# A nested set of seven quarter products in one of the seven block products of the down projection

## The chip, the cores and the metric

The kernel runs on one core of one Trainium2 chip. The metric is the device time of one execution in microseconds (us), the median of the runs shown. The engines are named as in the profile: PE multiplies matrices (PEld is its loading of weights), DVE and ACT work on vectors, POOL is a third engine that hardly matters here, and SP issues most DMA transfers.

## The reference

A decoder block over 1024 positions and 1024 channels in float32: a mixer (pooling and windowed attention), then an MLP. Only the MLP is touched by the change:

```python
h2 = _rmsnorm(x, g_mlp_pre[l])
ff = jnp.einsum('bsf,fd->bsd',
                jnp.square(jax.nn.relu(jnp.einsum('bsd,df->bsf', h2, w_up[l]))), w_down[l])
x = x + _rmsnorm(ff, g_mlp_post[l])
```

`w_up` is 1024 x 4096 and `w_down` 4096 x 1024. Below, f is the squared ReLU (1024 positions x 4096), the input of the down projection.

## The kernel before

**Three passes.** Every float32 matrix is split into a high part (a cast on ACT, L101) and a low part (a subtraction on DVE, L104), both in a rounded float32 format. A product is made in three passes of PE (`PASSES`, L32): high x high, high x low, low x high. A split's operand is ready when DVE has made its low part.

**Seven products for eight.** The matrix products of the MLP are made by blocks: the positions are halved, the columns are halved, the inner dimension is halved, and seven products of sums of blocks replace eight products of blocks. The seven are added up in a fixed scheme, in which later products are accumulated onto earlier ones in the PSUM banks where possible.

**The up part** goes over pairs of blocks of 128 columns of f. The class `Pairs` loads a pair's weights (L524, on SP's queue), makes their sums (L533 to L543), splits them (into tiles named wh and wx), and runs its seven products on PE (L584). The results are squared on ACT (L1613). The function `store` inside `up_close0` (L1615 to L1628) makes three sums of a pair's blocks of f, which the down part needs as left operands (s1, s2 and s4), and stores all to `f_dram` in DRAM. Its stores go to the same SP queue as the next pair's weight loads.

**The down part** is one list of steps: seven products in the order `PRODUCTS` (1, 5, 2, 3, 6, 7, 4), each in `NS` = 8 steps of 256 rows of the inner dimension. A step multiplies a left operand of 128 x 2 x 512 (the f sums, read back from `f_dram`, tile raw) by a right operand of the same size (blocks of `w_down` or differences of them, tiles B). `operands(i, s_)` issues the load, makes the difference of blocks of w where there is one, and splits both: the left into two slots of the pool wh (6 slots), the right into two of the pool ar (6 slots). It is called two steps ahead (`AHEAD`). `down_mm` then issues 24 matmuls of 128 x 128 by 128 x 512, that is 2 parts of the inner dimension x 4 tiles of 128 positions x 3 passes. A product is 192 matmuls. PSUM has two groups of four banks, "mm" and "at"; products 2 and 3 accumulate onto 1 and 5, the others start a group afresh.

Product 6, the fifth in the list, multiplies s2 by B22 - B11. After it, for each of the four tiles of positions, DVE adds the result to u (L2106), adds u to c12 (L2107) and to v (L2108), and multiplies c12 by a gain (L1991). Product 7 has DVE write B22 - B12 over B12's tile, and product 4 uses B21 - B11; its B21 blocks are loaded at L1966 into slots of the pool w (24 slots) that earlier blocks have left, and subtracted at L1967.

**Order.** Outside stretches whose order is written by hand, a scheduler of the framework places the instructions on each engine when the kernel is built. On the chip each engine then works through its list in that order, and an instruction that must wait (for data, or for a slot to be read for the last time) holds up all behind it on the same engine. That also holds for SP and its DMA issues.

Of the kernel before, what the change touches and what calls it, by code (L numbers as in the profile page):

```python
# [8 lines left out]
F32 = mybir.dt.float32  # L9
# [41 lines left out]
def block_kernel(ctx: ExitStack, tc, xt, x, consts, vecs, sinks, b_qkv, g_post, g_mlp, g_mlp_post,  # L51
# [1558 lines left out]
    def up_close0(m, f):  # L1610

        act.activation(f[:, 512:], f[:, 512:], AF.Relu)
        act.activation(f, f, AF.Square)  # L1613

        def store():  # L1615

            g = f_odd.pop(m + 1)
            t = g32([2, 512])
            s4 = (g32([S]) if m < 2 * NF0 else bcp.tile([P, S], F32, tag="bc", name=nm("s4")))[:, :512]
# [3 lines left out]
            dve.tensor_tensor(s4, g[:, :512], t[:, 1, :], ALU.subtract)  # L1623
# [7 lines left out]
    stores = []  # L1631

    def flush():
        while stores:
# [279 lines left out]
    dl = ctx.enter_context(tc.tile_pool(name="dl", bufs=16, reuse_waits="tile"))  # L1914

    def acc4(name):
        return [dl.tile([P, 512], F32, tag="acc", name=nm(name), bufs=16) for _ in range(4)]

    def raw_tile():
        return dl.tile([P, 2, 512], F32, tag="raw", name=nm("raw"), bufs=4)  # L1920
# [16 lines left out]
    def operands(i, s_):  # L1937

        if i == 1 and s_ in early_raw:
            ft, wt = early_raw[s_]  # L1940
        else:
            ft = stage([2, 512]) if (i, s_) == (1, 3) else raw_tile()
            nc.sync.dma_start(ft, f_block(A_OF[i], s_))
            if i == 1:
                resident("B11", s_)
                if s_ - 3 in early_raw:
                    resident("B11", s_ - 3)
                wt = res["B11", s_]
            elif i == 5:
                resident("B12", s_)  # L1950
                wt = res["B11", s_]
                dve.tensor_tensor(wt, res["B12", s_], wt, ALU.subtract)
            elif i == 2:
                wt = streamed("B21", s_)
            elif i == 3:
                resident("B22", s_)
                wt = res["B22", s_]
            elif i == 6:
                wt = res["B11", s_]
                dve.tensor_tensor(wt, res["B22", s_], wt, ALU.subtract)  # L1960
            elif i == 7:
                wt = res["B12", s_]
                dve.tensor_tensor(wt, res["B22", s_], wt, ALU.subtract)
            else:
                wt = rp.tile([P, 2, 512], F32, tag="w", name=nm("B21"))
                nc.sync.dma_start(wt, w_block("B21", s_))  # L1966
                dve.tensor_tensor(wt, wt, res["B11", s_], ALU.subtract)  # L1967
# [8 lines left out]
        opers[i, s_] = fo, wo_  # L1976

    def down_mm(i, s_, bs, after, order, last=(NS - 1, 1)):
        for s2, k2, t in order:
# [51 lines left out]
    def last_tile(i, n, b, order):  # L2031

        t = n - 4
        sums = small(2, "sq")
        b2 = bank("mm", [256])
        for h, o in ((0, b[:, :256]), (1, b2)):
            c = slice(h * 256, (h + 1) * 256)
            for s2, k2, _ in order:  # L2040
                fo, wo_ = opers[i, s2]
                for j, (fh, wh) in enumerate(PASSES):
                    pe.matmul(o, fo[fh][:, k2, t * P:(t + 1) * P], wo_[wh][:, k2, c],
                              start=h == 1 and k2 == 0 and j == 0, stop=k2 == 1 and j == 2, skip_group_check=h == 0)
# [20 lines left out]
    PRODUCTS = (1, 5, 2, 3, 6, 7, 4)  # L2065
    LATE = 3
# [5 lines left out]
    u, v, c11, c12 = acc4("u"), acc4("v"), acc4("c11"), acc4("c12")  # L2072
    banks = {}
    AHEAD = 2
    for j in range(1, AHEAD):
        operands(*steps[j])
    for j, (i, s_) in enumerate(steps):
        if j + AHEAD < len(steps):
            operands(*steps[j + AHEAD])
        if s_ == 0 and i not in (2, 3):  # L2080
            tag = "mm" if i in (5, 7) else "at"
            banks[i] = [bank(tag) for _ in range(4)]
        bs = banks[{2: 1, 3: 5}.get(i, i)]
# [4 lines left out]
        if i != 4 or s_ < NS - LATE:  # L2088
            down_mm(i, s_, bs, i in (2, 3), [(s_, k2, t) for k2 in range(2) for t in range(4)
                                             if (i, s_, t) != (4, NS - LATE - 1, 3)])  # L2090
            if s_ < NS - 1:
                continue
        elif s_ < NS - 1:
            continue
        for t in range(4):
# [7 lines left out]
            elif i == 3:  # L2103
                act.copy(c12[t], bs[t])
            elif i == 6:
                dve.tensor_tensor(u[t], u[t], bs[t], ALU.add)  # L2106
                dve.tensor_tensor(c12[t], c12[t], u[t], ALU.add)  # L2107
                dve.tensor_tensor(v[t], v[t], u[t], ALU.add)  # L2108
                fin_half(t, 1, c12[t])
# [104 lines left out]
```

## Time and profile before

| what | us |
|---|---|
| three runs | 1093.69, 1094.36, 1095.04 |
| median | 1094.36 |
| the profiled execution | 1093.78 |
| its span on the core | 1092.0 |
| PE busy | 1082.5 |
| DVE busy | 810.4 |
| ACT busy | 610.8 |

The span runs from the core's first instruction to its last; 1.8 us of the execution lie around it. In the trace's rows, a name such as `wh<-raw` is the tile written and the tiles read, `x12` is a run of twelve like instructions, and a bracket at the end says how long the engine stood idle before the row and what it waited for. An instruction's duration overlaps the next one's start by up to a tenth of a us on DVE and ACT, so the distance from start to start is what counts where instructions stand in a queue.

### The profile page before, as it was taken

The page shows a single profiled execution, that of the slowest core. Times are in us where ns is not written, and L with a number is a line of the kernel's source. Part 1 is how long each engine was busy: PE and PEld are TensorE (multiplying, and loading weights), DVE is VectorE, ACT ScalarE, POOL GpSimd, SP SyncE. Part 2 cuts the span into 40 slices and gives each one's busy share as a digit, 9 for nine tenths or more (in the row PEclk, how much of TensorE's full clock was granted, in tenths as well). Part 3 has the DMA queues.
Part 4 walks back from the last instruction along what each step waited for, and adds up shares of the span by engine and source line. Part 5 has one row for each costly group of instructions (what it writes and reads, how often), then busy time and mean ns, then how long its engine had stood idle before and what let it go on. Part 6 is the DMA issues. An engine that isn't in the chain of part 4 may idle for free.

```text
span 1092.0 us, 13883 instructions
## 1 busy us (share of the span) xinstructions
PE 1082.5 (99%) x5066; PEld 899.1 (82%) x5066; DVE 810.4 (74%) x1111; ACT 610.8 (56%) x1001; POOL 84.2 (8%) x142
## 2 busy tenths in 40 slices
PE   9999999999999999999999999999999999999997
PEld 8888888888888888888888888888888888888886
DVE  6689888999797887889867665655457866557685
ACT  7557886466654257457665564555346535435461
POOL 0344311100100012100000000000000000000000
PEclk9999999999999999999999999999999999999999
DMA  9858899679865776732565535345697886632622
GB/s 337 189 142 212 212 247 349 189 242 319 255 214 173 225 182 154 270 117 81 180 212 212 193 125 191 127 161 186 223 389 278 298 261 194 195 117 78 212 77 77
DMA packets 98612, 221.02 MB, mean 202 GB/s; under 512 B 10224, under 2 KB 27760, under 8 KB 98544
## 3 DMA queue, kind: packets, MB, share of 16 engines
q1 hardware_dynamic: 82256, 183.56, 50.2%
q0 software_dynamic: 10528, 16.78, 8.6%
q10 hardware_dynamic: 5760, 19.79, 4.8%
q8 instruction: 39, 0.64, 0.2%
q14 instruction: 29, 0.24, 0.1%
HBM read 158.24 MB, written 60.82 MB: 201 GB/s over the span
## 4 chain that ended last, share of the span: by engine, by line
PE 95%; DVE 2%; ACT 2%; DMA 0%; issue 0%; DVEq 0%; ACTq 0%; SPq 0%
PE mm L584 26%; PE at L584 18%; PE at L1982 15%; PE mm L1982 12%; PE mm L1516 5%; PE mm L495 3%; PE sc L183 2%; PE at L1244 2%; PE at L1516 2%; PE mm L192 2%; PE mm L1244 1%; PE mm L183 1%; PE mm L497 1%; PE sc L457 1%; PE sc L389 1%; PE at L1562 1%
## 5 line engine op out<-in xcount | busy, mean ns | idle before, releaser
L1982 PE MATMUL at<-ar,wh 128*128 128x512 f32 x696 | 159.0, 389 | 0.0
L1982 PEld LDWEIGHTS at<-ar,wh 128*128 128x128 f32 x696 | 130.6, 188 | 27.5 <-DVE ar L104 0.4
L1982 PE MATMUL mm<-ar,wh 128*128 128x512 f32 x576 | 131.0, 389 | 0.0
L1982 PEld LDWEIGHTS mm<-ar,wh 128*128 128x128 f32 x576 | 108.1, 188 | 22.5
L104 DVE TENSOR_TENSOR wh<-raw,wh 128x1024 fp32r<-128x1024 f32 x50 | 61.1, 1223 | 68.4 <-ACT wh L101 68.2
L101 ACT CAST wh<-raw 128x1024 fp32r<-128x1024 f32 x50 | 52.6, 1052 | 104.0 <-PE at L1982 51.6
L104 DVE TENSOR_TENSOR wh<-st,wh 128x512 fp32r<-128x512 f32 (+1 forms) x103 | 74.8, 736 | 30.0 <-ACT wh L101 25.5
L584 PE MATMUL mm<-T,wx 128*128 128x512 f32 x375 | 90.4, 389 | 0.0
L584 PEld LDWEIGHTS mm<-T,wx 128*128 128x128 f32 x375 | 70.4, 188 | 14.6
L584 PE MATMUL mm<-gr,wh 128*128 128x512 f32 x321 | 77.2, 391 | 0.0
L101 ACT CAST wh<-st 128x512 fp32r<-128x512 f32 (+2 forms) x102 | 65.7, 653 | 19.3 <-PE at L584 5.6
L584 PEld LDWEIGHTS mm<-gr,wh 128*128 128x128 f32 x321 | 59.9, 188 | 12.2
L584 PE MATMUL mm<-T,wh 128*128 128x512 f32 x267 | 66.1, 389 | 0.0
L104 DVE TENSOR_TENSOR ar<-B,ar 128x1024 fp32r<-128x1024 f32 x43 | 52.5, 1220 | 9.8 <-ACT ar L101 9.4
L584 PE MATMUL at<-gr,wh 128*128 128x512 f32 x243 | 59.0, 389 | 0.0
L584 PE MATMUL mm<-x,wh 128*128 128x512 f32 x240 | 58.9, 394 | 0.0
L584 PEld LDWEIGHTS mm<-T,wh 128*128 128x128 f32 x267 | 50.1, 188 | 10.4
L584 PEld LDWEIGHTS at<-gr,wh 128*128 128x128 f32 x243 | 45.6, 188 | 9.5
L584 PEld LDWEIGHTS mm<-x,wh 128*128 128x128 f32 x240 | 44.2, 188 | 9.6 <-ACT f L693 0.2
L584 PE MATMUL at<-T,wx 128*128 128x512 f32 x213 | 52.0, 389 | 0.0
L101 ACT CAST ar<-B 128x1024 fp32r<-128x1024 f32 x43 | 45.1, 1050 | 12.2 <-DMA B<-in_w_dn_dram 9.4
L584 PEld LDWEIGHTS at<-T,wx 128*128 128x128 f32 x213 | 40.0, 188 | 8.3
(510 smaller groups left out, 2127.0 us busy)
## 6 DMA issues: line engine op xcount, KB each, us to landing
raw<-f_dram SPq DMA_DIRECT2D x52, 512.0 KB, 3.9
B<-in_w_dn_dram SPq DMA_DIRECT2D x32, 512.0 KB, 6.7
f_dram<-g SPq DMA_DIRECT2D x28, 512.0 KB, 3.3
st<-in_w_up_dram SPq DMA_DIRECT2D x24, 512.0 KB, 4.7
g<-spill_dram SPq DMA_DIRECT2D x17, 512.0 KB, 5.7
f_dram<-g ACTq DMA_DIRECT2D x17, 512.0 KB, 2.6
st<-in_w_g_dram SPq DMA_DIRECT2D x16, 512.0 KB, 4.9
g<-in_w_up_dram SPq DMA_DIRECT2D x15, 512.0 KB, 5.9
```

The source lines that it names most:

```text
L101: act.copy(hi, src)
L104: eng.tensor_tensor(lo, src, f32(hi), ALU.subtract)
L183: pe.matmul(bq, xs_[k][n // 4][:, xh, n % 4 * P:(n % 4 + 1) * P], wq[k][:, h, :], start=k == 0 and j == 0, stop=k == NK - 1 and j == 2)
L192: pe.matmul(bkv_of(n), xs_[k][n // 4][:, xh, n % 4 * P:(n % 4 + 1) * P], wkv[k // 2][:, h, k % 2, :], start=k == 0 and j == 0 and not (joi ...
L389: pe.matmul(sb[:, kv, i, :nk], qt[r, qx, m * P:(m + 1) * P], kx[r, k0:k0 + nk], start=j == 0, stop=j == 2)
L457: pe.matmul(yb[:, kv], v[:, c:c + P], p[ph][:, 4 * kv:4 * kv + 4].rearrange("p i q -> p (i q)"), start=j < 2, stop=j >= len(mms) - 2)
L495: pe.matmul(bs[th], whi[:, k, :], rhs(k, hl, th), start=k == 0 and hl == 0, stop=False)
L497: pe.matmul(bs[th], wlo[:, k, :], rhs(k, 0, th), start=False, stop=k == nk - 1)
L584: pe.matmul(b, w[wh][:, kt, :], x_, start=not after and kt == 0 and j == 0, stop=kt == 3 and j == 2, skip_group_check=after)
L1244: pe.matmul(b, w[wh][:, kt, :], xo[xh][:, kt, :], start=not after and kt == 0 and j == 0, stop=kt == 1 and j == 2, skip_group_check=after)
L1516: pe.matmul(bs[t], Am[a][k][ah][:, t * P:(t + 1) * P], Wm[w][k][wh], start=not after and k == 0 and j == 0, stop=k == 3 and j == 2, skip_g ...
L1982: pe.matmul(bs[t], fo[fh][:, k2, t * P:(t + 1) * P], wo_[wh][:, k2, :], start=not after and s2 == 0 and k2 == 0 and j == 0, stop=(s2, k2) ...
```

## The change

Product 6 is itself made as seven products of quarters. s2 and B22 - B11 are halved once more in each direction: positions in two halves of 256, the inner rows of a step in two of 128, columns in two of 256. Per step there are seven products, each with 2 tiles of positions x 3 passes = 6 matmuls of 128 x 128 by 128 x 256: 42 in place of 24 of 512 columns.

- Left operands: the four quarters of s2 (`f1`) and three sums of quarters (`f2`). The sums run over two pairs of blocks of the up part. `store` makes the first half in even pairs (L1628) and the rest in odd pairs (L1633 to L1635), and puts them into the scratch tensor `spill`, 384 KB for each of the eight steps.
- Right operands: four quarters of B22 - B11, of which three are used as they are (`w1`), and four sums T (L2006 to L2008, `w2`).
- Splits of a step: f2 (768 columns), w2 (1024), w1 (512 and 256), f1 (1024), in place of two of 1024.
- Four of the seven quarter products start from zero in "at" banks; products 2, 3 and 4 accumulate onto three quarters of u that ACT copies into "mm" banks first (`ONTO`). `quarters_close` adds them up in u: one copy on ACT and eight additions on DVE. The four additions of L2106 go.
- Products 7 and 4 change their groups of banks ("at" for 7, "mm" for 4), and the tail's `b2` goes to "at".
- The last step and the closing are in an order written by hand, and product 7's operands are called for after it.

```diff
@@ store (up part)
+            if m // 2 % 2 == 0:
+                dve.tensor_tensor(s2[:, 256:], s2[:, :256], s2[:, 256:], ALU.subtract)
+                s2_even.append(s2)
+            else:
+                a = s2_even.pop()
+                e = g32([3, 256])
+                dve.tensor_tensor(e[:, 1, :], s2[:, 256:], a[:, 256:], ALU.subtract)
+                dve.tensor_tensor(e[:, 0, :], e[:, 1, :], a[:, :256], ALU.add)
+                dve.tensor_tensor(e[:, 2, :], s2[:, :256], e[:, 1, :], ALU.subtract)
+                q.dma_start(e_dram(m // 4), e)
             q.dma_start(fd[:, 4:6, :], t)
...
@@ operands
+        if i == QUARTERED:
+            quarters(s_, ft, wt)
+            return
...
+    def quarters(s_, ft, wt):
+        fs, w = raw_tile_of([3, 256]), halved(wt)
+        nc.sync.dma_start(fs, e_dram(s_))
+        tt = rp.tile([P, 4, 256], F32, tag="w", name=nm("T"))
+        dve.tensor_tensor(tt[:, 0:2, :], w[:, 1::2, :], w[:, 0:2, :], ALU.subtract)
+        dve.tensor_tensor(tt[:, 2, :], w[:, 3, :], tt[:, 0, :], ALU.subtract)
+        dve.tensor_tensor(tt[:, 3, :], w[:, 2, :], tt[:, 2, :], ALU.subtract)
+        f2, w2 = [wslot([3, 256]) for _ in range(2)], [ar([4, 256]) for _ in range(2)]
+        split(*f2, fs)
+        split(*w2, tt)
+        w1, f1 = [ar([4, 256]) for _ in range(2)], [wslot([4, 256]) for _ in range(2)]
+        for k in (slice(2, 4), slice(0, 1)):
+            split(w1[0][:, k, :], w1[1][:, k, :], w[:, k, :])
+        split(*f1, halved(ft))
+        opers[QUARTERED, s_] = f1, f2, w1, w2
+
+    PARTS = {1: (0, 0, 2, 0), 2: (0, 2, 2, 2), 3: (1, 2, 2, 3), 4: (0, 3, 3, 3), 5: (1, 0, 3, 0), 6: (1, 1, 3, 2),
+             7: (0, 1, 3, 1)}
+    ONTO = {2: (0, 0), 3: (0, 1), 4: (2, 0)}
...
+    def quarters_mm(s_):
+        o = opers[QUARTERED, s_]
+        order = (5, 6, 1, 7, 3, 2, 4) if s_ == 0 else (1, 6, 7, 5, 2, 3, 4) if s_ == NS - 1 else (5, 6, 3, 1, 2, 7, 4)
...
+        for q in order:
+            fs, fk, ws, wk = PARTS[q]
+            for t in range(2):
+                for j, (fh, wh) in enumerate(PASSES):
+                    pe.matmul(part[q][:, t, :], o[fs][fh][:, fk, t * P:(t + 1) * P], o[ws][wh][:, wk, :],
+                              start=q not in ONTO and (s_, t, j) == (0, 0, 0), stop=(s_, t, j) == (NS - 1, 1, 2),
+                              skip_group_check=q in ONTO)
+
+    def quarters_close():
+        (a, c), (d, e) = ([h[:, k] for k in range(2)] for h in (stage([2, 2, 256]), stage([2, 2, 256])))
+        act.copy(a, part[1])
+        dve.tensor_tensor(c, a, part[6], ALU.add)
+        dve.tensor_tensor(d, c, part[7], ALU.add)
+        dve.tensor_tensor(e, c, part[5], ALU.add)
+        w = block_of(u4, 2, 1)
+        dve.tensor_tensor(w, w, d, ALU.add)
+        dve.tensor_tensor(w, w, part[5], ALU.add)
+        for q, s in ((2, a), (3, e), (4, d)):
+            dve.tensor_tensor(block_of(u4, *ONTO[q]), s, part[q], ALU.add)
...
@@ the loop over steps
     for j, (i, s_) in enumerate(steps):
-        if j + AHEAD < len(steps):
+        closing = (i, s_) == (QUARTERED, NS - 1)
+        if j + AHEAD < len(steps) and not closing:
             operands(*steps[j + AHEAD])
...
+        if closing:
+            with tc.manual_schedule(engines=CORE):
+                quarters_mm(s_)
+                quarters_close()
+            operands(*steps[j + AHEAD])
...
             elif i == 6:
-                dve.tensor_tensor(u[t], u[t], bs[t], ALU.add)
                 dve.tensor_tensor(c12[t], c12[t], u[t], ALU.add)
```

Where the instructions stand now on the engines is seen in three places. First, DVE around the start of product 6, after the change (numbers behind names tell tiles apart; L1984 is the subtraction B21 - B11, which was L1967, and raw with 768 columns is the stored sum of quarters):

```order
L104 TENSOR_TENSOR wh_8204<-raw_8197,wh_8203 128x768
L104 TENSOR_TENSOR ar_8206<-T_8199,ar_8205 128x1024
L104 TENSOR_TENSOR ar_8212<-B_1085_7088,ar_8211 128x512
L104 TENSOR_TENSOR ar_8212<-B_1085_7088,ar_8211 128x256
L1984 TENSOR_TENSOR B_1422_9116<-B_1422_9116,B_1085_7088 128x1024
L104 TENSOR_TENSOR wh_8214<-raw_8194,wh_8213 128x1024
L1984 TENSOR_TENSOR B_1428_9153<-B_1428_9153,B_1092_7126 128x1024
L104 TENSOR_TENSOR wh_8255<-raw_8248,wh_8254 128x768
L104 TENSOR_TENSOR ar_8257<-T_8250,ar_8256 128x1024
```

The first four and the sixth row are step 0's splits, the last two belong to step 1: the second subtraction of L1984, with a load of its own in front of it, stands between them.

Second, DVE around the end of product 6, before and after. Before (the first two rows are the splits of product 7's step 1; u, c and v are the sums named above):

```order
L104 TENSOR_TENSOR wh_8476<-raw_8472,wh_8475 128x1024
L104 TENSOR_TENSOR ar_8478<-B_1119_7264,ar_8477 128x1024
L2106 TENSOR_TENSOR u_6979<-u_6979,at_8234 128x512
L2106 TENSOR_TENSOR u_6980<-u_6980,at_8235 128x512
L2107 TENSOR_TENSOR c_1063_6991<-c_1063_6991,u_6979 128x512
L2108 TENSOR_TENSOR v_6983<-v_6983,u_6979 128x512
L2107 TENSOR_TENSOR c_1064_6992<-c_1064_6992,u_6980 128x512
L2108 TENSOR_TENSOR v_6984<-v_6984,u_6980 128x512
L1991 TENSOR_TENSOR c_1063_6991<-c_1063_6991,bc_6964 128x512
```

After, with the eight additions of the closing (L2045 to L2052) and a B21 subtraction among them, and the splits of product 7's step 1 (wh_8837, ar_8839):

```order
L1984 TENSOR_TENSOR B_1460_9334<-B_1460_9334,B_1098_7162 128x1024
L2046 TENSOR_TENSOR st_8822<-st_8821,at_8330 128x512
L2047 TENSOR_TENSOR st_8822<-st_8821,at_8327 128x512
L2049 TENSOR_TENSOR u_7027<-u_7027,st_8822 128x2x256
L104 TENSOR_TENSOR wh_8837<-raw_8833,wh_8836 128x1024
L2050 TENSOR_TENSOR u_7027<-u_7027,at_8327 128x2x256
L2052 TENSOR_TENSOR u_7027<-st_8821,mm_8333 128x2x256
L2052 TENSOR_TENSOR u_7027<-st_8822,mm_8331 128x2x256
L2052 TENSOR_TENSOR u_7027<-st_8822,mm_8335 128x2x256
L104 TENSOR_TENSOR ar_8839<-B_1123_7309,ar_8838 128x1024
L2193 TENSOR_TENSOR c_1067_7036<-c_1067_7036,u_7027 128x512
```

Before, step 1 of product 7 was split ahead of the additions, and step 2's first split stood behind sixteen additions and multiplications, four for each tile. After, step 1's splits stand among the closing's additions, and twelve more additions and multiplications stand between them and step 2's.

Third, SP's queue in an odd pair of the up part, after the change (L1636 stores the sums of quarters, L524 loads weights):

```order
L1637 DMA f_dram<-g_5183 128x1024
L1638 DMA f_dram<-g_4624 128x1024
L1636 DMA spill_dram<-g_5189 128x768
L1639 DMA f_dram<-g_5184 128x512
L524 DMA g_5247<-in_w_up_dram 128x1024
```

The new store stands in front of the weight load that before followed directly upon three stores.

More of the change, by code (lines that the diff above doesn't have):

```diff
@@ L1629, in up_close0, with e_dram @@
         stores.append(store)
-    stores = []
+    stores, s2_even = [], []
+    def e_dram(s_):
+        return spill[s_][:, :768].rearrange("p (a b) -> p a b", b=256)
     def flush():
@@ L1916, in acc4, with raw_tile_of @@
     def acc4(name):
-        return [dl.tile([P, 512], F32, tag="acc", name=nm(name), bufs=16) for _ in range(4)]
+        return [dl.tile([P, 512], F32, tag="acc", name=nm(name), bufs=12) for _ in range(4)]
+    def raw_tile_of(shape):
+        return dl.tile([P] + shape, F32, tag="raw", name=nm("raw"), bufs=4)
     def raw_tile():
-        return dl.tile([P, 2, 512], F32, tag="raw", name=nm("raw"), bufs=4)
+        return raw_tile_of([2, 512])
     sq = sp.tile([P, 2, NT], F32, tag="fsq", name="fsq", bufs=1)
@@ L1976, in operands, with halved @@
         opers[i, s_] = fo, wo_
+    def halved(t):
+        return t.rearrange("p k (a b) -> p (k a) b", b=256)
+    def quarters(s_, ft, wt):
[13 more added lines that the diff above has]
+        opers[QUARTERED, s_] = f1, f2, w1, w2
@@ new lines, in block_kernel, with block_of @@
+    PARTS = {1: (0, 0, 2, 0), 2: (0, 2, 2, 2), 3: (1, 2, 2, 3), 4: (0, 3, 3, 3), 5: (1, 0, 3, 0), 6: (1, 1, 3, 2),
+             7: (0, 1, 3, 1)}
+    ONTO = {2: (0, 0), 3: (0, 1), 4: (2, 0)}
+    part = {}
+    def block_of(t4, r, j):
+        return t4[:, r:r + 2, j * 256:j * 256 + 256]
+    def quarters_mm(s_):
+        o = opers[QUARTERED, s_]
+        order = (5, 6, 1, 7, 3, 2, 4) if s_ == 0 else (1, 6, 7, 5, 2, 3, 4) if s_ == NS - 1 else (5, 6, 3, 1, 2, 7, 4)
+        if s_ == 0:
+            for q in (5, 6, 1, 7, 3, 2, 4):
+                part[q] = bank("mm" if q in ONTO else "at", [2, 256])
+                if q in ONTO:
+                    act.copy(part[q], block_of(u4, *ONTO[q]))
+        for q in order:
[5 more added lines that the diff above has]
+                              skip_group_check=q in ONTO)
@@ L2065, in block_kernel @@
     PRODUCTS = (1, 5, 2, 3, 6, 7, 4)
+    QUARTERED = 6
     LATE = 3
@@ L2071, in block_kernel @@
     steps = [(i, s_) for i in PRODUCTS for s_ in range(NS)]
-    u, v, c11, c12 = acc4("u"), acc4("v"), acc4("c11"), acc4("c12")
+    u4 = dl.tile([P, 4, 512], F32, tag="u4", name="u4", bufs=1)
+    u, v, c11, c12 = [u4[:, t, :] for t in range(4)], acc4("v"), acc4("c11"), acc4("c12")
     banks = {}
@@ L2077, in block_kernel @@
     for j, (i, s_) in enumerate(steps):
-        if j + AHEAD < len(steps):
+        closing = (i, s_) == (QUARTERED, NS - 1)
+        if j + AHEAD < len(steps) and not closing:
             operands(*steps[j + AHEAD])
-        if s_ == 0 and i not in (2, 3):
-            tag = "mm" if i in (5, 7) else "at"
+        if s_ == 0 and i in (1, 5, 7, 4):
+            tag = "mm" if i in (5, 4) else "at"
             banks[i] = [bank(tag) for _ in range(4)]
-        bs = banks[{2: 1, 3: 5}.get(i, i)]
+        bs = banks.get({2: 1, 3: 5}.get(i, i))
         if i == 5:
```

8 lines of the change are left out of this document (6 added, 2 removed).

## The prediction

> **What bounds the kernel now.** First the page: how full each engine is, and what the chain that ended last is made of.
>
> ```profile
> span 1092.0 us, 13883 instructions
> PE 1082.5 (99%) x5066; PEld 899.1 (82%) x5066; DVE 810.4 (74%) x1111; ACT 610.8 (56%) x1001; POOL 84.2 (8%) x142
> PE 95%; DVE 2%; ACT 2%; DMA 0%; issue 0%; DVEq 0%; ACTq 0%; SPq 0%
> ```
>
> PE is the bound over the whole span. Next, PE's waits, all of them, and the rows of the chain of waits for products 3, 6 and 7 of the down part:
>
> ```profile
> PE mm L201 <- DVE pad L160: 1.1, 1, 1.1
> PE sc L432 <- DVE s L421: 0.7, 1, 0.7
> PE sc L389 <- ACT yt L459: 0.3, 1, 0.3
> ...
> 910.57 43.52 PE mm L1982 x192
> 954.09 43.52 PE at L1982 x192
> 997.61 43.52 PE mm L1982 x192
> ```
>
> PE never waits in the up or the down part, so any wait there is new time, one for one. Then the windows of product 6 and product 7, to see how near DVE stands to PE:
>
> ```profile
> 953.93:997.45 43.52, 43.52 (x194) 36.04 (x193) 23.14 (x21) 16.56 (x19) 0.00 (x0) 1.00 0.41 120
> 997.45:1040.90 43.45, 43.45 (x193) 36.01 (x192) 34.23 (x48) 23.58 (x31) 0.00 (x0) 1.00 0.50 157
> ```
>
> Columns: PE, PEld, DVE, ACT, POOL, granted clock, DMA share, GB/s. In product 6 DVE works 23.1 of 43.5 us; product 7 begins with a pile of adds. Since PE has no slack to lose, the question is whether DVE can feed seven quarter products as fast as PE eats them.
>
> **PE's own time.** Product 6 goes from 192 matmuls of 512 columns to 8 x 42 = 336 of 256. A matmul of 512 costs 43.52/192 = 0.2267 us. For 256 columns in the same three passes:
>
> ```profile
> 33.07 1.60 PE L192 MATMUL mm<-wkv,x 128*128 128x256 f32 x12
> 34.50 2.91 PE L183 MATMUL sc<-wq,x 128*128 128x512 f32 x12
> 37.25 1.60 PE L192 MATMUL mm<-wkv,x 128*128 128x256 f32 x12
> 38.68 1.55 PE L183 MATMUL mm<-wh,x 128*128 128x512 f32 x6
> ...
> 1083.12 0.88 PE L2043 MATMUL at<-hold,hold 128*128 128x256 f32 x6
> 1083.84 0.88 PE L2043 MATMUL mm<-hold,hold 128*128 128x256 f32 x6
> ```
>
> From start to start, twelve take 1.43 us (0.119 each) and six take 0.72 (0.120). I take 0.1195: a step of 42 is 5.02 us (5.44 before) and the product 40.15, **-3.4 us**. If 256 columns cost exactly half of 512 (0.1133), it is 38.1, -5.4. The Trainium skill's page "TensorE: Matmul & The Clock Gate", section "Back-to-back issue gap", puts the isolated gap at 518 cycles for 512 columns and 262 for 256, that is 216 and 109 ns at 2.4 GHz, and by it the product would go from 41.4 to 36.7, an estimate of -4.7; the rows above are 5% and 9% longer than the page has it, so the smaller gain stands.
>
> **DVE's work in product 6.** Prices, and the spacing of queued instructions:
>
> ```profile
> L104 DVE TENSOR_TENSOR ar<-B,ar 128x1024 fp32r<-128x1024 f32 x43 | 52.5, 1220 | 9.8 <-ACT ar L101 9.4
> L104 DVE TENSOR_TENSOR wkv<-st,wkv 128x256 fp32r<-128x256 f32 x8 | 3.4, 420 | 0.2 <-ACT wkv L101 0.2
> ...
> 945.24 1.22 DVE L104 TENSOR_TENSOR ar<-B,ar 128x1024 fp32r<-128x1024 f32 x1
> 946.38 1.22 DVE L1967 TENSOR_TENSOR B<-B,B 128x1024 f32<-128x1024 f32 x1
> ...
> 1002.30 0.69 DVE L2108 TENSOR_TENSOR v<-v,u 128x512 f32<-128x512 f32 x1
> 1002.90 0.69 DVE L2107 TENSOR_TENSOR c<-c,u 128x512 f32<-128x512 f32 x1
> 1003.50 0.69 DVE L1991 TENSOR_TENSOR c<-c,bc 128x512 f32<-128x512 f32 x1
> ```
>
> Queued, 1024 columns are 1.14 apart (945.24 to 946.38) and 512 columns 0.60, both 0.08 to 0.09 under the duration. So 256 columns take about 0.34 (0.42 less 0.08), and 768, between 512 and 1024, about 0.87. A step of product 6 had two splits of 1024, 2.28 us. Now it has 768, 1024, 1024, 512 and 256: 0.87 + 1.14 + 1.14 + 0.60 + 0.34 = 4.1 us of PE's 5.02. The sums T (three more instructions a step) stand in front of product 6; in product 3 DVE is idle for 17.8 of 43.5 us, which hides them. But the subtractions B21 - B11 for product 4 move:
>
> ```profile
> 910.20:953.70 43.50, 43.50 (x194) 36.02 (x192) 25.67 (x24) 20.35 (x28) 0.00 (x0) 1.00 0.60 194
> ...
> 956.91 1.23 DVE L1967 TENSOR_TENSOR B<-B,B 128x1024 f32<-128x1024 f32 x1 [0.68 <-DMA B<-in_w_dn_dram]
> 962.74 1.23 DVE L1967 TENSOR_TENSOR B<-B,B 128x1024 f32<-128x1024 f32 x1
> ...
> L1967 DVE TENSOR_TENSOR B<-B,B x8: 1218/1220/1226, 908.3 to 1061.7; 128x1024 f32<-128x1024 f32 x8
> ```
>
> Two of the eight stood in product 6, five ahead of it; now five stand in it. Together 8 x 4.1 + 5 x 1.14 = 38.5, and with the two splits for product 7's first step 40.8, against PE's 40.15: DVE has no slack left. ACT makes five casts a step too, each shorter than the subtraction behind it, so it follows.
>
> **Where PE then waits.** Time t counts from PE's start on product 6 (953.93 above).
>
> First place, step 1. The second B21 subtraction stands ahead of step 1's splits, and its load cannot be issued before the first subtraction has freed the slot it goes to.
>
> ```profile
> DMA to landing us min/median/max: 3.3/4.6/5.2
> ```
>
> (The row is that of the eight B21 loads.) At 956.91 DVE already waited for such a load. By the order the first ends near -1.9, the second lands near 2.8 and ends at 4.0; the splits of f2 and of T behind it end at 6.05, where PE wants them at 5.14. PE loses about 1.2 us (0 with the fastest load, 1.8 with the slowest). Steps 2 to 6 then run at 5.02.
>
> Second place, the end of product 6. PE ends step 3 at 6.2 + 3 x 5.02 = 21.3; this frees the slots for the sums of step 5, whose splits start on DVE at 22.2 after a cast. From there DVE is never idle: steps 5 and 6 with a B21 subtraction each, 2 x 5.24, bring it to 32.7; then step 7's T, f2, a third subtraction, w1 and f1, 1.14 + 0.87 + 1.14 + 0.94 + 1.14 = 5.2, to 37.9, 38.1 with the waits between engines. Step 7 alone begins with part 1, which needs the last of these, f1, at 36.5: PE waits 1.6. So product 6 takes 40.15 + 1.2 + 1.6 = 43.0 against 43.52: nine tenths of the gain are gone.
>
> Third place, product 7, step 2. Before, its operands were ready just in time:
>
> ```profile
> 997.45 12.86 PE L1982 MATMUL mm<-ar,wh 128*128 128x512 f32 x56
> ...
> 1005.38 1.22 DVE L104 TENSOR_TENSOR wh<-raw,wh 128x1024 fp32r<-128x1024 f32 x1
> 1006.52 0.16 DVE L133 TENSOR_TENSOR sm<-fsq 128x4 f32<-128x4 f32 x1
> 1006.59 1.23 DVE L104 TENSOR_TENSOR ar<-B,ar 128x1024 fp32r<-128x1024 f32 x1
> ```
>
> They end at 1007.8, and PE wants step 2 at 997.45 + 2 x 5.44 = 1008.3. In after DVE does, from 38.1 on: the splits of product 7's step 0 (2.3), the eight instructions that close the quarters, one B21 subtraction and the splits of step 1 (8 x 0.60 + 3 x 1.14 = 8.2, and 0.4 for the last quarter, which PE ends only at 43.0: to 49.0), twelve additions and gains (12 x 0.60, to 56.2), and only then the two splits of step 2, which end at 58.5. PE, from 43.0, has run steps 0 and 1 and the four matmuls that need no low half by 43.0 + 10.88 + 0.9 = 54.8: **a wait of 3.7**. PE then stands 3.7 + 43.0 - 43.52 = **+3.2 us** behind before; I take +3.4 with the waits between engines on the way. After that DVE has 34 us of work in 43 and catches up.
>
> Bounds: DVE's chain from 22.2 to 58.5 sets this place, whatever PE waited before, so the end only moves with where the chain starts and how tightly it packs. Without the wait at step 1 it starts 1.2 earlier: +2.0. With semaphore delays of 0.05 on each of some twenty links: +4.5.
>
> **The up part.** Each pair of blocks gains one small subtraction or, in odd pairs, three and a store of 384 KB ahead of the next loads on SP's queue.
>
> ```profile
> 562.53 0.69 DVE L1623 TENSOR_TENSOR g<-g,g 128x512 f32<-128x512 f32 x1
> 563.76 1.13 SPq L524 DMA_DIRECT2D g<-in_w_up_dram  x1
> 569.62 0.69 DVE L533 TENSOR_TENSOR ws<-g 128x512 f32<-128x512 f32 x1 [5.20 <-DMA g<-in_w_up_dram]
> 572.15 0.69 DVE L104 TENSOR_TENSOR wx<-ws,wx 128x512 fp32r<-128x512 f32 x1
> 572.82 5.38 PE L584 MATMUL mm<-T,wx 128*128 128x512 f32 x23
> ```
>
> DVE already waits 5.2 us for the load issued behind the stores; the weights are ready at 572.84, and PE wants them when the twelve matmuls from 572.82 are through, 2.7 us later. Three subtractions (1.0), another instruction between them (0.6) and one DMA issue (some 0.4) put the load back 2 us, and the extra store adds between nothing and the 2 us that its transfer takes. So the load is 0.7 short of the slack to 1.3 beyond it, at the two or three odd pairs of this first stretch: **+0.8** in all, nearer the lower end since transfers side by side already fill these waits, from 0 to 3. Later pairs take 19 us of PE time and hide it.
>
> **Sum.** 3.4 + 0.8 = +4.2. The profiled execution took 1093.78, so 1098.0; it lies 0.58 under the median of 1094.36, and against that median it is 1098.6, of which I write 1098.5.
>
> **Rivals.** (a) *Not slower: DVE's chain is shorter than I reckon.* Place: from t = 22.2 to product 7's step 2, 36.3 us by my prices. Each us less takes one off the sum. If it is 2.0 shorter the kernel is within 0.2% of before; if it is 6.6 shorter and ends by 40.15 + 10.88 + 0.9 = 51.9, no wait is left and the whole -3.4 remains, 1091.0, or 1091.8 with the up part. For it: my prices for 768 and 256 columns are interpolated, and the load of B21 may land in 3.3 us, which starts the chain 1.2 earlier. Against it: some forty instructions stand in this chain, most of 512 or 1024 columns, whose spacing the trace shows. 1091 to 1096.5: 25 in 100, of which 8 for a gain of more than 2.2.
> (b) *Weight loads bound the short matmuls.*
>
> ```profile
> L1982 PEld LDWEIGHTS at<-ar,wh 128*128 128x128 f32 x696 | 130.6, 188 | 27.5 <-DVE ar L104 0.4
> L192 PEld LDWEIGHTS mm<-wkv,x 128*128 128x128 f32 x192 | 25.0, 191 | 1.2
> ```
>
> A load lasts 188 ns; if each matmul had to wait for its own, the product would take 336 x 0.188 = 63.2, +19.7, near 1118. Against it: L192's matmuls have 191 ns loads and run at 0.119, so loads overlap. 1 in 100.
>
> (c) *The clock falls.* The granted clock reads 1.00 in both windows above, in which PE never paused; the wait of 3.7 us is longer than any in this trace. If it dropped to half speed after this wait, for as long as the wait, PE would lose half of 3.7 more, near 1100.3. The Trainium skill's page "TensorE: Matmul & The Clock Gate", section "What's actually happening", says that an idle window of some 3.4 us halves the clock until as long a busy one has passed; no run here shows it. 7 in 100.
> (d) *The up part waits more*: at each odd pair of the first stretch the full 1.3, or its loads pushed on, +3 in place of +0.8: 1100.7. 8 in 100.
>
> **How the numbers follow.** My forecast, 1096.6 to 1100 with DVE's chain as the limit, has 59 in 100. The range takes in (c), (d) and the slow ends (4.5 + 3 on 1094.4, 1101.9) and the upper half of (a): 1094.0 to 1102.0. A difference of 0.2%, 2.2 us, is about what a measurement of this kernel can tell from none: faster 0.08, same 0.17, slower 0.75.
>
> **What would show it.** PE's product 6 should last about 43 us with two waits on DVE, of 1.2 at step 1 and 1.6 at step 7; DVE in it over 95% busy; in product 7 one wait of some 3.7 us, 10.9 us in, on a split of L104; in the up part waits below 1.5 us around 575 to 610 for weights. Had PE waited at no place of products 6 and 7, or a matmul of 256 columns taken other than 0.12, the forecast's working would be wrong.

## The result and the profile after

| | before | after |
|---|---|---|
| median of the runs, us | 1094.03 (4 runs, 1093.46 to 1095.04) | 1100.11 (4 runs, 1098.76 to 1101.53) |
| the profiled execution, its span, us | 1093.78, 1092.0 | 1099.66, 1097.9 |

A fourth run moves the median of before from 1094.36 to 1094.03. The ratio is 1.0055, with a 95% interval of 1.0042 to 1.0067: 6.1 us slower, where 4.2 was forecast. The page of after, in the lines that answer to those of before:

```profile
span 1097.9 us, 14345 instructions
PE 1082.1 (99%) x5210; PEld 904.9 (82%) x5210; DVE 850.0 (77%) x1195; ACT 626.1 (57%) x1029; POOL 85.2 (8%) x142
PE 91%; DVE 5%; ACT 2%; DMA 1%; issue 1%; DVEq 0%; ACTq 0%; SPq 0%
```

PE's busy time hardly fell although its matmuls should need 3.2 us less, and the chain of waits now holds 5% of DVE where it held 2%. PE's waits, as the profile counts them:

```profile
PE at L2058 <- DVE ar L104: 3.2, 1, 3.2
PE mm L201 <- DVE pad L160: 1.1, 1, 1.1
PE at L2038 <- DVE wh L104: 0.7, 1, 0.7
PE mm L2038 <- DVE ar L104: 0.7, 1, 0.7
PE at L2038 <- DVE ar L104: 0.7, 1, 0.7
```

L2038 are the quarter products and L2058 the other products of the down part. The four waits of 3.2 and 0.7 are new, all on splits of DVE, none in the up part. Where they stand in PE's timeline (some rows between them left out):

```profile
953.80 3.04 PE L2038 MATMUL at<-ar,wh 128*128 128x256 f32 x24
...
958.84 1.60 PE L2038 MATMUL at<-ar,wh 128*128 128x256 f32 x12
960.27 1.18 PE L2038 MATMUL mm<-ar,wh 128*128 128x256 f32 x6
...
980.72 0.28 PE L2038 MATMUL mm<-ar,wh 128*128 128x256 f32 x1
981.73 0.86 PE L2038 MATMUL mm<-ar,wh 128*128 128x256 f32 x5 [0.73 <-DVE ar L104]
...
990.35 0.28 PE L2038 MATMUL at<-ar,wh 128*128 128x256 f32 x1
991.36 0.39 PE L2038 MATMUL at<-ar,wh 128*128 128x256 f32 x1 [0.73 <-DVE ar L104]
992.49 2.90 PE L2038 MATMUL at<-ar,wh 128*128 128x256 f32 x22 [0.75 <-DVE wh L104]
...
997.39 11.97 PE L2058 MATMUL at<-ar,wh 128*128 128x512 f32 x52
1012.60 33.60 PE L2058 MATMUL at<-ar,wh 128*128 128x512 f32 x140 [3.23 <-DVE ar L104]
1046.03 28.72 PE L2058 MATMUL mm<-ar,wh 128*128 128x512 f32 x126
```

Product 6 lasts from 953.80 to 997.39, 43.59 us where it lasted 43.52: the gain is used up inside it. DVE (the third engine in the row) is busy for 38.83 us of it, where it had 23.14 before:

```profile
953.80:997.39 43.59, 41.34 (x338) 40.53 (x336) 38.83 (x45) 30.97 (x43) 0.00 (x0) 1.00 0.86 286
```

Product 7 takes 48.64 us to 1046.03, 5.1 more than before. The wait at 1012.60 explains 3.4 of that (the 52 matmuls ahead of it need until 1009.18). The rest is in the 140 matmuls behind it: at 0.2267 each they need 31.7 us and took 33.4. The windows behind the wait show why (the figure of interest is the granted clock, the third from the end):

```profile
1012.60:1014.00 1.40, 1.40 (x3) 1.15 (x4) 1.40 (x4) 1.40 (x2) 0.00 (x0) 0.50 0.76 228
1014.00:1016.00 2.00, 2.00 (x6) 1.57 (x5) 2.00 (x3) 2.00 (x3) 0.00 (x0) 0.50 0.67 180
1016.00:1018.00 2.00, 2.00 (x10) 1.65 (x10) 2.00 (x5) 0.13 (x1) 0.00 (x0) 1.00 0.71 200
```

For 3.4 us, from 1012.60 to 1016.00, PE ran at half its clock, which costs 1.7. The chain's last piece of product 4 starts at 1046.19 where it started at 1041.13: 5.06 us of the 5.9 by which the spans differ. The other 0.8 lies behind the last DVE instruction, in the last stores of these two executions.

### The profile page after: what moved, and what is told of

The parts are those of the page before. It is cut to its first block, busy times and chain, and to the rows that moved or that the text cites. A ratio compares the mean times of both kernels' runs of the same rounds, so it can differ in the third digit from the quotient of the medians.

```text
span 1097.9 us, 14345 instructions
## 1 busy us (share of the span) xinstructions
PE 1082.1 (99%) x5210; PEld 904.9 (82%) x5210; DVE 850.0 (77%) x1195; ACT 626.1 (57%) x1029; POOL 85.2 (8%) x142
## 4 chain that ended last, share of the span: by engine, by line
PE 91%; DVE 5%; ACT 2%; DMA 1%; issue 1%; DVEq 0%; ACTq 0%; SPq 0%
PE mm L584 26%; PE at L584 18%; PE at L2058 11%; PE mm L2058 11%; PE mm L1516 5%; PE mm L495 3%; PE sc L183 2%; PE at L1516 2%; PE at L1244 2%; PE mm L192 2%; PE mm L1244 1%; PE mm L183 1%; PE mm L497 1%; PE at L2038 1%; PE sc L457 1%; DVE wh L104 1%
## 5 line engine op out<-in xcount | busy, mean ns | idle before, releaser
L2058 PE MATMUL at<-ar,wh 128*128 128x512 f32 x552 | 127.5, 393 | 3.2 <-DVE ar L104 3.2
L2058 PEld LDWEIGHTS at<-ar,wh 128*128 128x128 f32 x552 | 104.7, 190 | 25.4 <-DVE ar L104 3.7
L2058 PE MATMUL mm<-ar,wh 128*128 128x512 f32 x528 | 120.5, 389 | 0.0
L2058 PEld LDWEIGHTS mm<-ar,wh 128*128 128x128 f32 x528 | 99.1, 188 | 20.6
L101 ACT CAST wh<-raw 128x1024 fp32r<-128x1024 f32 (+1 forms) x58 | 59.3, 1022 | 87.3 <-PE at L2058 35.3
L104 DVE TENSOR_TENSOR wh<-st,wh 128x512 fp32r<-128x512 f32 (+1 forms) x103 | 74.9, 738 | 37.8 <-ACT wh L101 33.4
L104 DVE TENSOR_TENSOR wh<-raw,wh 128x1024 fp32r<-128x1024 f32 (+1 forms) x58 | 68.7, 1185 | 43.9 <-ACT wh L101 43.6
L104 DVE TENSOR_TENSOR ar<-B,ar 128x1024 fp32r<-128x1024 f32 (+2 forms) x51 | 50.9, 1010 | 8.6 <-ACT ar L101 8.3
L101 ACT CAST ar<-B 128x1024 fp32r<-128x1024 f32 (+2 forms) x51 | 44.1, 880 | 15.0 <-DMA B<-in_w_dn_dram 5.8
```

The costliest lines, as they stand in the source:

```text
L101: act.copy(hi, src)
L104: eng.tensor_tensor(lo, src, f32(hi), ALU.subtract)
L2058: pe.matmul(bs[t], fo[fh][:, k2, t * P:(t + 1) * P], wo_[wh][:, k2, :], start=not after and s2 == 0 and k2 == 0 and j == 0, stop=(s2, k2) ...
```

## The experiments

My theory (theory 1) was: DVE is the cause, in two ways. Its load in product 6 keeps PE waiting there; the order of its instructions at product 7's step 2 makes the long wait; and this wait takes the clock down. The rivals were the up part, the short matmuls themselves, and a clock that falls for other reasons. Each comparison below is with the kernel before on the same chip, whose median was 1093.7 to 1093.9 each time. Line numbers differ by a few from kernel to kernel: the quarter products are L2038 or L2044, the other products of the down part L1992, L1996, L2058 or L2064.

**up_only**: the kernel before with the change's `store` alone. One half of s2 is altered in place there, as in the change, and product 6 reads it so.

> Only the up part's share of the change on the kernel before: the sums of quarters are made and stored, and never read; product 6 stays one block product. Theory 1 (in the changed trace PE never waits in the up part, so the extra subtractions and the eight stores of 384 KB are hidden): the same as before within 0.5 us, no PE wait in the up part. Rival (part of the 6 us lies there, in stretches where a wait is hidden by the way the trace counts): +0.8 to +3 us.

1094.97 for 1093.86, ratio 1.0008 (1.0000 to 1.0017). No PE wait in the up part in its trace; the one new wait stands in product 1, behind a late load of weights:

```profile
802.41 21.61 PE L1996 MATMUL at<-ar,wh 128*128 128x512 f32 x94 [0.54 <-DVE ar L104]
```

So theory and rival could not be told apart by this run; no_sums below returns to it.

**adds_later**: the twelve additions and gains go one step later in the code, and the outputs made from them (`fin_out`) move by a step with them.

```diff
+    due = {}
...
+        if j in due:
+            due.pop(j)()
...
-        if i == 7 and 1 <= s_ <= 4:
-            fin_out(s_ - 1, (c11, c12))
+        if i == 7 and 2 <= s_ <= 5:
+            fin_out(s_ - 2, (c11, c12))
...
+        if i == 6:
+            def sums():
+                for t in range(4):
+                    dve.tensor_tensor(c12[t], c12[t], u[t], ALU.add)
+                    dve.tensor_tensor(v[t], v[t], u[t], ALU.add)
+                    fin_half(t, 1, c12[t])
...
+            due[j + 1] = sums
+            continue
...
-            elif i == 6:
-                dve.tensor_tensor(c12[t], c12[t], u[t], ALU.add)
-                dve.tensor_tensor(v[t], v[t], u[t], ALU.add)
-                fin_half(t, 1, c12[t])
```

> The changed kernel with one move: the twelve additions and gains of DVE that stand ahead of the splits of product 7, step 2 come behind them. Theory 1 (DVE's order at this place makes PE wait 3.2 us, and the wait takes the clock down for 3.4 us, 1.7 us more): that wait falls to nothing, the granted clock stays 1.00, and the time falls by 4.5 to 5.2 us, to 1094.9 to 1095.6; the waits inside product 6 stay (2.2 us). A wait of up to 0.5 us at step 3 is possible. Rival (the clock drop is the chip's and comes at this place whatever PE waited): only 3.2 us come back, 1096.9. Rival (the twelve additions only pass the wait on to step 3): 0 to 1 us come back.

1093.63 for 1093.86, ratio 1.0001 (0.9992 to 1.0010): 6.5 us under the change. Product 7 runs through, with the clock at 1.00:

```profile
989.82 0.38 PE L2038 MATMUL at<-ar,wh 128*128 128x256 f32 x1 [0.33 <-DVE ar L104]
990.95 2.90 PE L2038 MATMUL at<-ar,wh 128*128 128x256 f32 x22 [0.75 <-DVE wh L104]
993.68 2.32 PE L2038 MATMUL mm<-ar,wh 128*128 128x256 f32 x18
995.85 44.07 PE L2058 MATMUL at<-ar,wh 128*128 128x512 f32 x192
...
995.85:1039.75 43.90, 43.83 (x194) 35.97 (x193) 39.86 (x56) 24.95 (x33) 0.00 (x0) 1.00 0.65 209
```

More came back than the 4.5 to 5.2 expected. The long wait and the clock make 5.1 of it. In this execution, the fastest of its 11, the wait at step 5 of product 6 was absent, too, and product 7 started 1.5 us earlier than in the change. DVE's order inside product 6 is the same in both. But the third B21 load, issued at 972.45 in the change and at 972.34 here, landed after 6.2 us there, and soon enough here for its subtraction to start at 977.18 in place of 978.71. Nothing in the two traces ties this to the moved additions, so these 1.5 us are not shown to be the order's.

**b21_pool**: the subtractions for product 4 go to POOL (`dve.tensor_tensor` becomes `pool.tensor_tensor` in the line of B21 - B11).

> The changed kernel with the eight subtractions B21 - B11 on POOL in place of DVE. Theory 1 (DVE's chain through product 6 is what PE waits for): 5.7 us of DVE work leave product 6, PE's waits at steps 5 and 7 go, product 6 takes 40.3 to 40.6 us, product 7's step 2 is late by only 1.1 us (0 to 2), the clock stays up, and the time is 2 to 3 us under the kernel before, 1091.0 to 1092.2. Rival (POOL's subtractions slow DVE or hold the loads of SP's queue as long as DVE's did): the waits stay and the time is 1096 or more. Rival (the 256-column matmuls themselves keep product 6 at 43 us): no gain in product 6, only at step 2 of product 7.

1107.02 for 1093.86, ratio 1.0122 (1.0109 to 1.0136): far worse, by the first rival, and in a way I had not priced. POOL and DVE side by side:

```profile
985.70 5.82 POOL L1984 TENSOR_TENSOR B<-B,B 128x1024 f32<-128x1024 f32 x2 [2.62 <-DVE wh L104]
...
984.76 1.21 DVE L104 TENSOR_TENSOR ar<-T,ar 128x1024 fp32r<-128x1024 f32 x1
985.90 3.42 DVE L104 TENSOR_TENSOR wh<-raw,wh 128x1024 fp32r<-128x1024 f32 x1
989.25 3.16 DVE L104 TENSOR_TENSOR ar<-B,ar 128x512 fp32r<-128x512 f32 x2
```

POOL needs some 2.9 us for each of these two (2.4 at the least in this run) where DVE needs 1.2, and a DVE subtraction that starts beside it takes 3.42 instead of 1.22. DVE thus loses 2.2 us to save 1.14. The Trainium skill's page "SBUF — State Buffer", section "Who interferes with whom", says that a DVE instruction with two inputs from SBUF contends with a GpSimd instruction that reads SBUF, that the port pair they share is an exclusive lock, and that the order of issue decides who blocks. These rows agree with it: DVE starts 0.20 us behind POOL and ends 2.2 us late.

The longer waits of PE in this run add the clock to the price: behind two waits of 3.13 us it reads 0.50. Behind a wait of 1.48 us it stays up:

```profile
962.61 0.86 PE L2038 MATMUL mm<-ar,wh 128*128 128x256 f32 x5 [1.48 <-DVE ar L104]
...
962.61:964.41 1.80, 1.80 (x15) 1.80 (x16) 1.80 (x3) 1.02 (x1) 0.00 (x0) 1.00 0.67 202
```

**both**: adds_later and b21_pool together.

> Both moves: B21 - B11 on POOL, and the twelve additions behind the splits of product 7's step 2. Theory 1: no PE wait is left in products 6 and 7; the whole gain of the shorter matmuls stays, 3.2 us (336 x 0.120 = 40.3 for 43.5): 1090.5 to 1091.2. Rival (the gain of the quarter products is not there, PE loses it in between its short matmuls): 1093 to 1094.5.

1103.70, ratio 1.0091 (1.0077 to 1.0105). It only repeats that POOL is no place for this work; a test of DVE's load had to keep the work on DVE.

**b21_late**: adds_later, with seven of the subtractions pinned behind splits of product 7, still on DVE.

```diff
-        eng.tensor_tensor(lo, src, f32(hi), ALU.subtract)
+        return eng.tensor_tensor(lo, src, f32(hi), ALU.subtract)
...
+    lows, PIN = {}, (None, 3, 3, 4, 4, 5, 6, 7)
...
-                dve.tensor_tensor(wt, wt, res["B11", s_], ALU.subtract)
+                if PIN[s_] is None:
+                    dve.tensor_tensor(wt, wt, res["B11", s_], ALU.subtract)
+                else:
+                    with tc.issue_after(lows[7, PIN[s_]].ins):
+                        dve.tensor_tensor(wt, wt, res["B11", s_], ALU.subtract)
...
-        split(*wo_, wt)
+        lows[i, s_] = split(*wo_, wt)
```

> The kernel of the run adds_later, with seven of the eight subtractions B21 - B11 (still on DVE) placed by hand behind splits of product 7, steps 3 to 7, in place of inside product 6 and its closing. Theory 1 (DVE's load through product 6 is what PE waits for there): product 6 has at most one wait under 0.3 us and lasts 40.4 to 40.8 us; the time is 1 to 1.6 us under adds_later and 1.5 us or more under the kernel before, 1091.5 to 1092.3. Rival (the moved subtractions, or the B21 loads that now wait for their slots on SP's queue, hold up product 7 or 4): new PE waits there, and a time of 1093 or more. Rival (PE's 256-column matmuls are longer by themselves): product 6 stays above 41.5 without waits.

1091.34 for 1093.70, ratio 0.9977 (0.9969 to 0.9986): 2.4 us under the kernel before, the first version that is faster than that kernel and the change. It is 2.3 under adds_later, where 1 to 1.6 was expected. PE's timeline, and the windows of products 6 and 7:

```profile
989.83 3.01 PE L2044 MATMUL at<-ar,wh 128*128 128x256 f32 x23 [0.22 <-DVE ar L104]
994.85 43.86 PE L2064 MATMUL at<-ar,wh 128*128 128x512 f32 x192
...
953.93:994.85 40.92, 40.70 (x338) 40.40 (x337) 34.31 (x41) 31.05 (x43) 0.00 (x0) 1.00 0.84 282
994.85:1038.55 43.70, 43.70 (x195) 35.97 (x194) 42.81 (x58) 24.21 (x31) 0.00 (x0) 1.00 0.68 220
```

Product 6 lasts 40.92 us (40.4 to 40.8 expected) with one wait of 0.22, and DVE's load in it is 34.3 us (38.8 in the change). The moved work fills product 7, where DVE is busy for 42.8 of 43.7 us and still in time: there it delays nothing that PE wants.

**last_order** and **b21_late_order**: product 6's last step begins with parts 5 and 6, on adds_later and on b21_late.

```diff
-        order = (5, 6, 1, 7, 3, 2, 4) if s_ == 0 else (1, 6, 7, 5, 2, 3, 4) if s_ == NS - 1 else (5, 6, 3, 1, 2, 7, 4)
+        order = (5, 6, 1, 7, 3, 2, 4) if s_ == 0 else (5, 6, 1, 7, 2, 3, 4) if s_ == NS - 1 else (5, 6, 3, 1, 2, 7, 4)
```

> The kernel of the run adds_later, with product 6's last step in the order of parts 5, 6, 1, 7, 2, 3, 4 in place of 1, 6, 7, 5, 2, 3, 4, so that the operands which DVE splits last (f1 and w1) are needed 1.4 us later. Theory 1: the wait at step 7 (1.5 us with the time that PE needs to start again) shrinks to nothing, 1.0 us under adds_later, 1092.4 to 1092.9. Rival (the additions that close the quarters come later by as much, and product 7 waits for its banks): no change within 0.5 us.

1093.93 for 1093.70, ratio 1.0003 (0.9993 to 1.0012): no gain. The wait at step 7 is down to 0.3, but two others have come up behind it in product 7:

```profile
992.33 1.46 PE L2038 MATMUL at<-ar,wh 128*128 128x256 f32 x10 [0.30 <-DVE wh L104]
...
1002.79 11.18 PE L2058 MATMUL at<-ar,wh 128*128 128x512 f32 x48 [0.47 <-DVE ar L104]
1014.71 26.59 PE L2058 MATMUL at<-ar,wh 128*128 128x512 f32 x116 [0.74 <-DVE ar L104]
```

The time is the rival's, but not its cause: they wait for splits, not for banks. As long as DVE's chain is the limit, a wait taken away at one place comes back at the next.

> Both: the subtractions placed in product 7 and 4, and the last step beginning with parts 5 and 6, on the kernel of the run adds_later. Theory 1: product 6 at 40.3 us with no wait, the whole 3.2 us of the shorter matmuls less what the up part may cost (0 to 0.9): 1090.7 to 1091.8. Rival (the gain is bounded elsewhere): no better than the better of its two parts.

1091.75 for 1093.70, ratio 0.9980 (0.9971 to 0.9988): as b21_late within the intervals, as the rival said, since no wait worth naming was left to take away. Theory 1's 1090.7 to 1091.8 holds this time too, so the run does not decide between the two.

**b21_late_only**: the subtractions pinned as in b21_late, the additions where the change has them.

> The changed kernel with the B21 subtractions placed behind splits of product 7 as in the run b21_late, but with the twelve additions ahead of the splits of product 7's step 2 as in the change. Theory 1 (two causes that add: DVE's load keeps PE waiting inside product 6, DVE's order keeps it waiting at product 7's step 2): product 6 at 40.9 us as in b21_late, and one wait of about 3.1 us at step 2, since DVE ends that split 14.9 us after PE starts product 7 and PE wants it after 11.8; 1094.4 if the clock stays, 1096.1 if it falls behind this wait. Rival (the load was the only cause and the order costs nothing once the load is gone): 1091.3 to 1092.

1096.45 for 1093.73, ratio 1.0023 (1.0014 to 1.0033). As expected with the fall of the clock: one wait at the same place, and half the clock behind it.

```profile
1009.97 33.63 PE L2064 MATMUL at<-ar,wh 128*128 128x512 f32 x140 [3.01 <-DVE ar L104]
...
1011.00:1013.00 2.00, 2.00 (x7) 1.52 (x6) 2.00 (x5) 2.00 (x3) 0.00 (x0) 0.50 0.78 211
```

With this the four combinations are complete:

| median, us | B21 subtractions in product 6 | in product 7 and 4 |
|---|---|---|
| additions ahead of step 2's splits | 1100.11 (the change) | 1096.45 |
| additions behind them | 1093.63 | 1091.34 |

The order costs 5.1 (right column) to 6.5 us (left), the load 2.3 to 3.7. The medians come from different chips, on which the kernel before differs by up to 0.3 us, and the change has 4 runs only. The two costs do not simply add: 1.4 us are left over, which no run explains. In the two traces of the left column about as much lies in product 6, at the late B21 load, so 5.1 is the better figure for the order.

**no_sums**: b21_late without the up part's new work.

> The kernel of the run b21_late without the up part's new work: no sums of quarters are made or stored, so that product 6 reads other numbers from the scratch tensor; all else is the same. Theory 1 (the up part's work is hidden): the same as b21_late within 0.5 us, 1090.9 to 1091.8. Rival (it costs what the run up_only showed at the middle of its interval): 0.9 us less, 1090.4.

1091.81 for 1093.73, ratio 0.9980 (0.9972 to 0.9989), beside b21_late's 0.9977: leaving the work out gains nothing that can be seen, though the two intervals are too wide to exclude 0.8. The traces say it more directly. In the chain of waits, products 1 and 5 start at 779.89 and 823.41 in the change and at 779.70 and 823.53 before, so in that execution the up part cost nothing. So the 0.9 of up_only is not the price of the stores in the change; whether its late load in product 1 belongs to that kernel's own schedule or to chance was not followed further.

**dose** and **dose2**: the kernel before with idle subtractions on DVE ahead of one split in each of four products, one run of each.

> The kernel before with idle work on DVE (3, 4, 5 and 7 subtractions of 1024 columns into a scratch tile) ahead of one split in step 4 of the products 5, 2, 3 and 6, so that PE waits four times, between nothing and some 5 us, with the computation unchanged. Theory 1 (a PE wait between the 1.5 us that left the clock alone and the 3.1 us that did not takes it down, for 3.4 us, 1.7 us more): the granted clock reads 0.5 behind each wait over about 3 us and 1.0 behind each shorter one. Rival (the clock fell for another reason, the place or the load): it stays 1.0 behind all four, or falls behind short ones.

> The kernel of the run dose with more idle work on DVE (6, 6, 8 and 9 subtractions ahead of one split in step 4 of the products 5, 2, 3 and 6), since only waits of 0.3 and 1.2 us came out of it; about 2.5 us in product 2 and 3.5 in product 6 are meant. Theory 1: the granted clock falls to 0.5 for 3.4 us behind a wait over a bound that lies between 1.5 and 3.1 us, and stays 1.0 behind shorter ones. Rival: it stays, or falls behind short ones as well.

The first gave waits of only 0.28 and 1.23 us, with the clock at 1.00 behind both. The second gave four. Behind them stand the windows of the 1.8 us after the first, the third, the fourth and the second of them:

```profile
849.17 22.75 PE L1992 MATMUL mm<-ar,wh 128*128 128x512 f32 x92 [3.00 <-DVE ar L1983]
895.12 21.15 PE L1992 MATMUL at<-ar,wh 128*128 128x512 f32 x92 [0.53 <-DVE ar L1983]
941.42 22.75 PE L1992 MATMUL mm<-ar,wh 128*128 128x512 f32 x92 [2.49 <-DVE ar L1983]
991.59 23.25 PE L1992 MATMUL at<-ar,wh 128*128 128x512 f32 x92 [4.76 <-DVE ar L1983]
...
849.17:850.97 1.80, 1.80 (x5) 1.42 (x6) 1.80 (x2) 1.30 (x3) 0.00 (x0) 0.54 0.80 232
941.42:943.22 1.80, 1.80 (x4) 1.45 (x5) 1.80 (x2) 0.00 (x0) 0.00 (x0) 0.52 0.84 272
991.59:993.39 1.80, 1.80 (x4) 1.49 (x5) 1.80 (x2) 0.00 (x0) 0.00 (x0) 0.50 1.01 368
895.12:896.92 1.80, 1.80 (x8) 1.50 (x9) 1.39 (x2) 1.05 (x1) 0.00 (x0) 1.00 0.86 282
```

The clock falls behind waits of 2.49, 3.00 and 4.76 us and not behind 0.53. It is the wait that does it: these waits stand in three other products, in a kernel without the change. DVE's load is not the cause either: the waits of 3.00 and 0.53 both stand behind six idle subtractions, and only the longer one takes the clock down. The 92 matmuls behind each wait need 20.9 us and took 22.6 behind 3.00 and 2.49, 1.7 more, and 23.1 behind 4.76, 2.2 more.

## Why the prediction was right, and where it was off

**Right: the bound and the sign.** PE's time was to be lost to DVE, and it was; adds_later and b21_late take the two causes away one by one, and with both gone the gain of the short matmuls appears.

**Right: the short matmuls.** A step of 42 took 953.80 to 958.84, 5.04 us (5.02 in the sum). The whole -3.4 never shows, but b21_late gets 2.6 of it (40.92 for 43.52).

**Off, first place: step 1.** A wait of 1.2 us was forecast there (6.05 less 5.14, the prediction's own figures, is 0.9), and the profile counts none; six matmuls from 960.27 to 961.29 took 0.3 longer than their 0.72. The step that failed is the load: the second B21 subtraction was to start at t = 2.8 and began at 1.8, so the splits of f2 and T behind it were done at 958.8, when PE wanted them. The wait showed up at step 5 instead, behind the third B21 load, which I had taken to be there in time. DVE's rows:

```profile
955.57 1.23 DVE L1984 TENSOR_TENSOR B<-B,B 128x1024 f32<-128x1024 f32 x1 [2.65 <-DMA B<-in_w_dn_dram]
...
978.71 1.23 DVE L1984 TENSOR_TENSOR B<-B,B 128x1024 f32<-128x1024 f32 x1 [0.91 <-DMA B<-in_w_dn_dram]
...
1001.68 1.22 DVE L104 TENSOR_TENSOR ar<-B,ar 128x1024 fp32r<-128x1024 f32 x1
1002.82 0.68 DVE L2193 TENSOR_TENSOR c<-c,u 128x512 f32<-128x512 f32 x1
...
1010.12 1.21 DVE L104 TENSOR_TENSOR wh<-raw,wh 128x1024 fp32r<-128x1024 f32 x1
1011.25 0.15 DVE L133 TENSOR_TENSOR sm<-fsq 128x4 f32<-128x4 f32 x1
1011.33 1.22 DVE L104 TENSOR_TENSOR ar<-B,ar 128x1024 fp32r<-128x1024 f32 x1
```

**Right, second place: the last step.** 1.6 us were forecast; the two waits of 0.73 and 0.75 cost 1.9, as each takes some 0.2 more than the profile counts as idle (990.35 to 991.36 is 1.01 for a matmul of 0.12). Product 6 came to 43.6 where 43.0 was worked out. (1.2 and 1.6 are five sixths of the gain of 3.4, not nine tenths; in the trace all of it went.)

**Off: a DVE without a pause.** The forecast had DVE over 95% busy in product 6. It was busy for 38.83 of 43.59 us, 89%; the rest is waits for B21 loads (the first two rows above) and for ACT's casts (0.69, 0.36 and 0.94). The stretch that was to run without a pause from t = 22.2 to 58.5 ran from 21.8 to 58.75, with the wait of 0.91 for the third load in it.

**Right, third place: product 7's step 2.** Its split was to end at t = 58.5 and ended at 1012.55, t = 58.75. The wait was 3.2 by the profile, 3.4 in PE's time, against 3.7. The twelve additions stand between 1002.82 and 1010.12, as in the order.

**Wrong: the clock had only 7 in 100.** Rival (c) happened in full, on top of the forecast, and cost 1.7 us of the 5.06 by which PE fell behind. The row for it was missing: no wait in the trace of before was long enough to show one. The Trainium skill's page that the prediction named, "TensorE: Matmul & The Clock Gate", section "What's actually happening", was the one hint: with a forecast wait of 3.7 us beside the 3.4 of its idle window the rival should have been the likelier of the two cases.

**Luck in the size.** That +4.2 came as near as it did to the 5.06 of the traces is partly luck. The missing 1.7 of the clock and 0.6 more lost in product 6 stand against 0.8 for the up part that did not come and a loss at product 7's step 2 that was 0.5 smaller than allowed for (3.4, where 3.7 and 0.2 for waits on the way were in the sum). The last 0.8 of the 5.9 between the spans lies in the last stores, for which the sum had no term. 1100.11 is just outside the 1096.6 to 1100 of the forecast proper and inside the whole range, which was drawn to take in (c).

**Wrong: the up part.** +0.8 was in the sum. The trace of the change shows no PE wait there and product 5 starting no later than before, and no_sums is 0.3 us slower than b21_late where 0.8 faster was to be expected (each with 0.9 to either side). The slack of 2.7 us there was enough. Without this term and with the clock the sum would have been +5.1, beside the 5.06 of the chain of waits.

## What to carry to other kernels

Fewer or shorter matmuls gain time only if the engines that prepare their operands have the time to do so: count, per step, the instructions of each engine and the work that the scheduler moves in between, and look at the first steps after the change for operands that were just in time. What stands ahead of a needed split in an engine's queue costs as much as what the split itself takes, so work that nobody waits for, here additions and later products' subtractions, belongs behind it. A wait of PE of some 2.5 us or more is priced with the clock that it takes down, here 1.7 us behind waits of 2.49 to 3.23 us and 2.2 behind 4.76.

## What the runs showed of the hardware

- **The clock falls behind shorter waits than expected.** It fell behind waits of PE of 2.49, 3.00, 3.01, 3.13, 3.23 and 4.76 us, and stayed up behind 0.53, 1.23 and 1.48 (dose, dose2, b21_pool, b21_late_only and the change), for 3.4 us in the change. So the bound lies between 1.48 and 2.49 in these runs. The Trainium skill's page "TensorE: Matmul & The Clock Gate", section "What's actually happening", gives an idle window of about 3.4 us for the fall; the runs show it after 2.49 already, and the measurement decides.
- **POOL beside DVE blocks it.** A subtraction of 1024 float32 columns took some 2.9 us on POOL, and DVE's took 3.42 instead of 1.22 beside it (b21_pool), so an idle POOL was no spare engine for DVE here.
